# Streaming encoder step: the order of the last convolution norms, the queue of their stores, and the place of the samples' loads

## The chip, the cores and the metric

The kernel runs on one core of a Trainium2 chip. The core has four compute engines that each work through a queue of their own in order: TensorE (PE: matrix products and transposes; its weight loads are listed as PEld), VectorE (DVE), ScalarE (ACT) and GpSimd (POOL). They wait for each other by semaphores. SyncE (SP) computes nothing here and issues most DMA transfers, also in order; GpSimd's queue issues some. The metric is the device time of one execution in microseconds (us), lower is better.

## The reference

One step of a streaming encoder layer, in float32, for a new stream of 2048 frames (the prompt) and for 8 running streams of 16 frames (the samples). What this case touches is the first sub-layer, the mixer. Attention and convolution share one input projection:

```python
proj = h @ w_in
q, k, v, u_val, u_gate = jnp.split(proj, [D_ATT, 2 * D_ATT, 3 * D_ATT, 3 * D_ATT + D_CONV], axis=-1)
...
att = band_attention(pad(q), k_ext, v_ext, key_valid, rel_bias)[:, :T]
...
u = u_val * jax.nn.sigmoid(u_gate)
u_ext = jnp.concatenate([conv_buf, u], axis=1)
c = lax.conv_general_dilated(u_ext, conv_w[:, None, :], window_strides=(1,), padding="VALID",
    dimension_numbers=("NWC", "WIO", "NWC"), feature_group_count=D_CONV) + conv_b
c = jax.nn.silu(layernorm(c, cln_g, cln_b))
...
y = jnp.concatenate([att, c], axis=-1) @ w_out
```

D_MODEL is 1024, D_ATT and D_CONV are 512, the convolution is 31 frames wide, and there are 8 heads of 64 with a relative-position bias in the softmax. A prompt query sees its own chunk of 64 keys and 8 chunks before it; a sample sees 256 cached keys and its 16 new ones. Cross-attention into 256 memory tokens and a SwiGLU network of 2816 follow. The step also returns the new key, value and convolution rows.

## The kernel before

Tokens stand in tiles of 128: tiles 0 to 15 are the prompt, and one more (the sample tile) holds the 8 x 16 frames of the samples. The program has stages: memory projections, `phase_proj` (the mixer's input projection and the convolution), `attention`, the output projection, cross-attention, and the feed-forward network. Matrix products are exact to float32 by a split of each operand in a high and a low part, three products each (`mm3`, lines 283 to 285).

`phase_proj` runs over three groups of tiles. The last group is tiles 12 to 15 and the sample tile. In each group come values, then the convolution's inputs, then `qk(which, j, blk, x)`: keys (which = 1) and queries (which = 0) for the channel block j of 4, for x = 0 (three prompt tiles, products 384 wide) and x = 1 (the rest, 256 wide). The results go to DRAM arrays `ks` and `qs` (L717), and keys also to the output (L716, L714).

The depthwise convolution is done on VectorE (L523), and for the samples on ScalarE and GpSimd (L532, L533). Its steps stand in the Python lists `vq` and `pq`; `pump` draws one step at a time while the products are written. When all four channel blocks of a group (`cts`) are done, `conv_norm` does a LayerNorm and swish on each tile. Its steps, in order, are:

- four transposes on PE (L538), statistics on DVE (L540, L542), the reciprocal root on POOL (L298, L301);
- normalization on DVE (L546);
- four transposes back on PE (L550), scale and bias four times on ACT (L553, into buffer `z`, of which there are two), tanh on ACT (L556), the last product on DVE (L557), and the store of `cs[t]` to DRAM by SP (L558), 256 KB.

The tile's norms of the last group were put in `vq` in pairs: those of tiles 12 to 15 as the group begins, that of the sample tile at the end.

In `attention`, units of one head and one tile follow one another: `scores` (L856) with its softmax (L793 on DVE, L795 on ACT), transposes (L873) and products with the values (L886). With head h, the generator `sample(h)` handles sample h for all heads: it loads the cached keys `kt` (L800), cached values `vc` (L802) and new values `vn` (L804), appends the new keys on POOL (L806), lays out queries on DVE (L811), and computes scores (L816), softmax with the bias `bs` (L793, 272 wide), and products (L835). `head_load` (L780, L781) brings a head's queries, keys and values into SBUF; for head h + 1 it is written six units into head h. The bias `bs` is loaded once in eight parts of 16 rows (L899), to a place that the convolution's buffers had; the memsets L903 and the buffer of L890 are on such places too.

A scheduler of the tile framework puts the instructions of each engine into one order before the run. The program bends it by `issue_after(ins)`: an instruction within it comes behind `ins` in the order. PSUM is in tagged regions: in `phase_proj`, "mm" for products, "tr" for transposes and "ca" for the convolution's sums.

## Time and profile before

| | us |
|---|---|
| time before, median of 3 runs | 2971.57 (2968.06 to 2972.08) |
| the profiled execution's own time | 2970.86 |
| its span, first to last instruction | 2969.1 |
| TensorE busy in the span | 2877.8 (97%) |
| VectorE busy | 2076.6 (70%) |
| GpSimd busy | 1367.9 (46%) |
| ScalarE busy | 1308.7 (44%) |

The span starts with the first instruction and ends with the last; the execution's own time has 1.8 us around it. A row of a timeline has the start, the duration, the engine, the line, the operation, what it writes and reads, how often it ran in a row, and in brackets how long the engine had been idle before it and what ended the idle time. "SPq" marks an instruction that SP issues for a DMA; its duration is that of the issue, not of the transfer. The last convolution products of `phase_proj` are at about 615 us, and attention begins at 641 us.

### The profile page before, as it was taken

The numbers are of one execution on the slowest core, as the hardware profiler recorded it, in microseconds if no ns is written. First come the engines' busy times: TensorE is split into PE (matmuls) and PEld (weight loads), VectorE is DVE, ScalarE is ACT, GpSimd is POOL, SyncE is SP. The second block draws the span as 40 slices with busy tenths as digits, with TensorE's granted clock in tenths as the row PEclk, the third lists the DMA queues.
The fourth block names the chain that finished last, engine by engine and source line by source line (L and its number), as shares of the span: only waits on it lengthen the run. The fifth ranks groups of instructions, "written<-read, shape, count | busy, mean of one in ns | idle before, by whom it ended". The sixth has DMA issues, their size and how long they took to land.

```text
span 2969.1 us, 45382 instructions
## 1 busy us (share of the span) xinstructions
PE 2877.8 (97%) x16740; PEld 2628.1 (89%) x16740; DVE 2076.6 (70%) x3024; ACT 1308.7 (44%) x2661; POOL 1367.9 (46%) x1247
## 2 busy tenths in 40 slices
PE   8999999979989998999999999999999999999998
PEld 8999999968978776888879999999999999888786
DVE  6697795958985334445459888787888998546655
ACT  4535354648973223333334333433344444433433
POOL 0268395720022223145447656365656775424413
PEclk9999999989999999999999999999999999999999
DMA  8635255557845664223355333644434446756654
GB/s 307 245 114 179 91 167 161 169 154 188 214 144 175 229 219 164 76 96 126 112 172 196 138 114 133 200 155 152 145 121 160 148 143 211 242 172 221 226 193 165
DMA packets 198474, 500.04 MB, mean 168 GB/s; under 512 B 18981, under 2 KB 87085, under 8 KB 189923
## 3 DMA queue, kind: packets, MB, share of 16 engines
q1 hardware_dynamic: 187931, 461.09, 48.2%
q0 software_dynamic: 10320, 36.05, 3.1%
q8 instruction: 131, 2.15, 0.3%
q14 instruction: 92, 0.75, 0.1%
HBM read 365.97 MB, written 141.81 MB: 171 GB/s over the span
## 4 chain that ended last, share of the span: by engine, by line
PE 42%; DMA 3%; POOL 2%; DVE 2%; issue 1%; ACT 0%; DVEq 0%; SPq 0%; POOLq 0%; ACTq 0%
PE psb L285 13%; PE psb L284 13%; PE psb L283 13%; PE psb L291 1%; DMA sbf<-in_w_down_dram 1%; DMA sbf<-x 1%; POOL sbf L1500 1%; PE psb L1355 1%; DMA sbf<-hn 1%; POOL sbf L340 0%; DVE sbr L1378 0%; DMA hn<-sbf 0%; DVE flexb L1440 0%; DVE sbr L1561 0%; DVE sbx L1378 0%
## 5 line engine op out<-in xcount | busy, mean ns | idle before, releaser
L283 PE MATMUL psb<-sbr 128*128 128x384 f32 (+3 forms) x2808 | 942.1, 337 | 3.3 <-ACT sbr L319 1.1
L284 PE MATMUL psb<-sbr 128*128 128x384 f32 (+3 forms) x2356 | 805.6, 342 | 2.4 <-DVE sbr L320 2.4
L285 PE MATMUL psb<-sbr 128*128 128x512 f32 (+3 forms) x1848 | 632.7, 344 | 2.2 <-DVE sbr L1561 2.2
L283 PEld LDWEIGHTS psb<-sbr 128*128 128x128 f32 x2808 | 530.5, 189 | 32.5 <-ACT sbr L1357 1.7
L285 PE MATMUL psb<-sbr,sbx 128*128 128x384 f32 (+2 forms) x1484 | 476.8, 322 | 0.0
L284 PEld LDWEIGHTS psb<-sbr 128*128 128x128 f32 x2356 | 445.0, 189 | 29.4 <-DVE sbr L320 2.7
L285 PEld LDWEIGHTS psb<-sbr 128*128 128x128 f32 x1848 | 348.0, 189 | 30.6 <-DVE sbr L1561 4.2
L291 PE MATMUL psb<-sbr 128*128 128x512 f32 x1226 | 304.6, 397 | 12.5 <-ACT sbr L319 8.5
L1378 DVE TENSOR_TENSOR sbr<-sbf,sbr 128x512 fp32r<-128x512 f32 x258 | 263.3, 1023 | 38.0 <-ACT sbr L1377 37.2
L291 PEld LDWEIGHTS psb<-sbr 128*128 128x128 f32 x1226 | 227.8, 189 | 64.1 <-ACT sbr L319 9.0
L1377 ACT CAST sbr<-sbf 128x512 fp32r<-128x512 f32 x258 | 159.3, 620 | 277.3 <-PE psb L284 235.7
L285 PEld LDWEIGHTS psb<-sbr,sbx 128*128 128x128 f32 x1484 | 280.6, 189 | 0.2
L523 DVE SCALAR_TENSOR_TENSOR psb<-sbf,psb 128x768 f32<-128x768 f32 (+1 forms) x290 | 264.3, 912 | 6.2
L1561 DVE TENSOR_TENSOR sbr<-sbf,sbr 128x384 fp32r<-128x384 f32 (+1 forms) x231 | 163.0, 728 | 96.6 <-ACT sbr L1560 95.3
L278 POOL TENSOR_TENSOR sbx<-sbf,sbr 128x1024 fp32r<-128x1024 f32 x60 | 152.1, 2537 | 78.3 <-ACT sbr L277 73.7
L1560 ACT CAST sbr<-sbf 128x384 fp32r<-128x384 f32 (+1 forms) x231 | 111.0, 497 | 167.6 <-PE psb L284 146.2
L1500 POOL TENSOR_TENSOR sbf<-sbf 128x512 f32<-128x512 f32 x77 | 107.3, 1399 | 166.6 <-DMA sbf<-in_w_down_dram 165.1
L533 POOL TENSOR_TENSOR flexb<-flexb,flexb 128x128 f32<-128x128 f32 (+1 forms) x180 | 167.2, 929 | 21.3 <-ACT flexb L532 11.7
L283 PE MATMUL psb<-sbr,sbx 128*128 128x384 f32 (+1 forms) x524 | 170.5, 327 | 0.7 <-ACT sbr L1357 0.7
L1377 ACT CAST sbx<-sbf 128x512 fp32r<-128x512 f32 x153 | 94.7, 620 | 160.5 <-PE psb L284 151.1
L1378 DVE TENSOR_TENSOR sbx<-sbf,sbx 128x512 fp32r<-128x512 f32 x153 | 151.8, 994 | 15.0 <-ACT sbx L1377 14.6
L1372 POOL TENSOR_TENSOR sbf<-sbf 128x512 f32<-128x512 f32 x66 | 97.4, 1476 | 109.5 <-DVE sbr L1378 51.3
(322 smaller groups left out, 5910.4 us busy)
## 6 DMA issues: line engine op xcount, KB each, us to landing
af<-flexb SPq DMA_DIRECT2D x33, 1344.0 KB, 6.2
sbf<-in_w_down_dram SPq DMA_DIRECT2D x154, 256.0 KB, 3.7
sbf<-af SPq DMA_DIRECT2D x90, 384.0 KB, 4.0
sbf<-in_w_gate_dram SPq DMA_DIRECT2D x66, 512.0 KB, 3.3
sbf<-in_w_up_dram SPq DMA_DIRECT2D x66, 512.0 KB, 3.3
sbf<-x SPq DMA_DIRECT2D x49, 512.0 KB, 3.9
sbf<-in_w_in_dram SPq DMA_DIRECT2D x48, 512.0 KB, 3.9
sbr<-ks SPq DMA_DIRECT2D x28, 512.0 KB, 10.1
```

Of the source, the lines that this page charges most:

```text
L278: self.lo_engine.tensor_tensor(lo[:, :], wf[:, :], hi[:, :].bitcast(F32), ALU.subtract)
L283: nc.tensor.matmul(ps, lh, rh, start=start, stop=False, **kw)
L284: nc.tensor.matmul(ps, lh, rl, start=False, stop=False, **kw)
L285: nc.tensor.matmul(ps, ll, rh, start=False, stop=stop, **kw)
L291: nc.tensor.matmul(y[o], l, r[:, o * 512:(o + 1) * 512], start=start and x == 0, stop=stop and x == 2)
L523: nc.vector.scalar_tensor_tensor(acc if w < CW - 1 else o, src(w), cwt[:, j, w:w + 1], acc, ALU.mult, ALU.add)
L533: nc.gpsimd.tensor_tensor(o, o, v, ALU.add)
L1377: nc.scalar.copy(hs[j][:, :], src[j])
L1378: nc.vector.tensor_tensor(ls[j][:, :], src[j], hs[j][:, :].bitcast(F32), ALU.subtract)
L1500: nc.gpsimd.tensor_tensor(acc[:, :], acc[:, :], q[:, :], ALU.add if s > 0 else ALU.subtract)
L1560: nc.scalar.copy(ch[:, m], a[:, x, m])
L1561: nc.vector.tensor_tensor(cl[:, m], a[:, x, m], ch[:, m].bitcast(F32), ALU.subtract)
```

## The change

The change does three things.

First, the five norms of the last group are no longer drawn from `vq`. When the last channel block's projections begin, the lists of convolution steps are emptied, the five `conv_norm` generators are made, with a PSUM tag "nt" of their own, and their steps are written behind each of the four last `qk` calls: one step each of tiles 12 and 13 behind the first; a second step of these and the first of tiles 14 and 15 behind the second; and so on. `issue_after` puts them behind the last product written so far.

Second, the `cs` stores of these five norms are issued by GpSimd's queue instead of SP's.

Third, a sample's three loads are issued on SP behind the last load of its head (for sample 0: behind the last store of `ks` or `qs` written).

```diff
-        nc.tensor.matmul(ps, ll, rh, start=False, stop=stop, **kw)
+        self.last_product = nc.tensor.matmul(ps, ll, rh, start=False, stop=stop, **kw)
...
-        ps_mm = ps_tr = Region().lay(self.ps, 0, ("mm", 2, 4), ("tr", 2, 2), ("ca", 4, 1))
+        ps_mm = ps_tr = Region().lay(self.ps, 0, ("mm", 2, 4), ("tr", 2, 2), ("ca", 4, 1)).lay(self.ps, 12, ("nt", 2, 2))
...
-        def conv_norm(t, cts, off):
-            pt = self.t(ps_tr, [P, 4, P], F32, "tr")
+        def conv_norm(t, cts, off, tag="tr"):
+            pt = self.t(ps_tr, [P, 4, P], F32, tag)
...
-            nc.sync.dma_start(self.cs[t], z[:, :, :].rearrange("p a b -> p (a b)"))
+            (nc.sync if tag == "tr" else nc.gpsimd).dma_start(self.cs[t], z[:, :, :].rearrange("p a b -> p (a b)"))
...
-            if last:
-                vq += pairs(tiles[:-1], cts)
-
...
-                nc.sync.dma_start(dst[:, :, col:col + npc].rearrange("c p n -> p c n"),
-                                  sp[:, :, :npc].bitcast(F32))
+                self.last_load = nc.sync.dma_start(dst[:, :, col:col + npc].rearrange("c p n -> p c n"),
+                                                   sp[:, :, :npc].bitcast(F32))
...
+            if last:
+                while vq or pq:
+                    pump(vq or pq, 1)
+                norms = [conv_norm(t, cts, i * P, "nt") for i, t in enumerate(tiles)]
+
+            def behind(*steps):
+                with self.tc.issue_after(self.last_product.ins):
+                    for i, n in steps:
+                        for _ in range(n):
+                            next(norms[i], None)
+
             for x in range(2):
                 for w in (1, 0):
                     qk(w, 3, blks[w], x)
+                    if last:
+                        behind(*[((0, 1), (1, 1)), ((0, 2), (1, 2), (2, 1), (3, 1)),
+                                 ((2, 2), (3, 2), (4, 1)), ((4, 2),)][2 * x + 1 - w])
...
-            if last:
-                vq += pairs(tiles[-1:], cts, len(tiles) - 1)
...
-        nc.sync.dma_start(v2[:, a:b, :].bitcast(F32), self.vs[h // 4][:, h % 4, a:b, :])
+        return nc.sync.dma_start(v2[:, a:b, :].bitcast(F32), self.vs[h // 4][:, h % 4, a:b, :])
...
-            nc.sync.dma_start(kt[:, :, :PAST], A["cache_att_kt"][s].rearrange("p (c k) -> p c k", k=PAST))
             vc = self.t(pool, [P, 2, 512], F32, "vc", 2)
-            nc.sync.dma_start(vc[:, :, :], A["cache_att_v"][s].rearrange("(b p) d -> p b d", p=P))
             vn = self.t(pool, [DEC_S, 512], F32, "vn", 2)
-            nc.sync.dma_start(vn[:, :], self.vsamp[s * DEC_S:(s + 1) * DEC_S, :])
+            with self.tc.issue_after(self.last_load.ins):
+                nc.sync.dma_start(kt[:, :, :PAST], A["cache_att_kt"][s].rearrange("p (c k) -> p c k", k=PAST))
+                nc.sync.dma_start(vc[:, :, :], A["cache_att_v"][s].rearrange("(b p) d -> p b d", p=P))
+                nc.sync.dma_start(vn[:, :], self.vsamp[s * DEC_S:(s + 1) * DEC_S, :])
...
-                    self.head_load(h + 1, heads[h + 1], 0, NPT)
+                    self.last_load = self.head_load(h + 1, heads[h + 1], 0, NPT)
```

Line numbers move: after the change L707 is L704, L714 is L711, L716 is L713, L717 is L714, L780 is L789, L781 is L790, L800 is L812, L802 is L813, L804 is L814, L806 is L816, L811 is L821, L816 is L826, L820 is L830, L856 is L866, L873 is L883, L899 is L909, L903 is L913, and the softmax L793 and L795 are L802 and L804. Lines up to 558 keep their numbers.

The order of the instructions moves in three places. On TensorE, where the convolution ends before the change, the norms' transposes (L538, L550) of tiles 12 to 15 stand together, and 48 products of 384 columns (L283 to L285) come behind them:

```order
L538 MATMUL psb<-ident_73,flexb_157 128x128 x2
L550 MATMUL psb<-ident_73,flexb_153 128x128 x8
L538 MATMUL psb<-ident_73,flexb_157 128x128 x8
L550 MATMUL psb<-ident_73,flexb_153 128x128 x4
L707 MATMUL psb<-ident_73,sbf 128x128 x3
L283 MATMUL psb<-sbr 128x384
L284 MATMUL psb<-sbr 128x384
L285 MATMUL psb<-sbr,sbx 128x384
```

After the change, on TensorE at the end of the projections and the beginning of attention, the rows are these (L866 are scores):

```order
L285 MATMUL psb<-sbr,sbx 128x256
L866 MATMUL psb<-sbr 128x256 x4
L866 MATMUL psb<-sbr 128x128 x2
L550 MATMUL psb<-ident_73,flexb_153 128x128 x4
L538 MATMUL psb<-ident_73,flexb_157 128x128 x4
L550 MATMUL psb<-ident_73,flexb_153 128x128 x4
L538 MATMUL psb<-ident_73,flexb_157 128x128 x4
L866 MATMUL psb<-sbr 128x512 x2
L866 MATMUL psb<-sbr 128x384 x2
L704 MATMUL psb<-ident_73,sbf 128x128
L866 MATMUL psb<-sbr 128x384 x2
L538 MATMUL psb<-ident_73,flexb_157 128x128 x4
```

All products are now ahead, and the norms stand among the scores of the first units; ahead of the piece shown, only the first transposes of tiles 12 and 13 stand among the 256 products. In both programs 18 score products stand ahead of sample 0's scores.

On GpSimd, at the same place, before the change:

```order
L301 TENSOR_TENSOR flexb_157<-flexb_157,mhalf_78 128x1
L298 TENSOR_SCALAR flexb_157<-flexb_157 128x1
L301 TENSOR_TENSOR flexb_157<-flexb_157,mhalf_78 128x1
L806 COPY sbf<-flexb_153 128x4x16 x2
L298 TENSOR_SCALAR flexb_157<-flexb_157 128x1
L301 TENSOR_TENSOR flexb_157<-flexb_157,mhalf_78 128x1
L903 MEMSET flexb_153 128x128 x2
L806 COPY sbf<-flexb_153 128x4x16
L820 TENSOR_SCALAR flexb_153<-flexb_153,flexb_157 128x272
```

On GpSimd after the change (cs_32 to cs_36 are the rows of tiles 12, 13, 14, 15 and the sample tile):

```order
L558 DMA cs_32_104<-flexb_153 128x512
L298 TENSOR_SCALAR flexb_157<-flexb_157 128x1
L301 TENSOR_TENSOR flexb_157<-flexb_157,mhalf_78 128x1
L558 DMA cs_33_105<-flexb_153 128x512
L913 MEMSET flexb_153 128x128 x2
L816 COPY sbf<-flexb_153 128x4x16
L558 DMA cs_34_106<-flexb_153 128x512
L558 DMA cs_35_107<-flexb_153 128x512
L558 DMA cs_36_108<-flexb_153 128x512
L830 TENSOR_SCALAR flexb_153<-flexb_153,flexb_157 128x272
```

The five stores now stand in this queue, and the copy of a sample's new keys (L816) is ahead of the last three; that copy writes a buffer that sample 0's scores read.

On SP, from the value load of head 1 (L781), before the change:

```order
L781 DMA sbr<-vs_18_90 128x2048
L717 DMA ks_17_89<-sbf 128x2x384
L558 DMA cs_35_107<-flexb_153 128x512
L780 DMA sbr<-qs_10_82 64x2048
L780 DMA sbr<-ks_14_86 64x2048 x2
L716 DMA out_dram<-sbf 128x512 x3
L717 DMA qs_13_85<-sbf 128x2x384
L717 DMA ks_17_89<-sbf 128x2x128
L716 DMA out_dram<-sbf 128x512
L714 DMA out_dram<-sbf 8x16x512
L802 DMA flexb_157<-in_cache_att_v_dram 128x2x512
L780 DMA sbr<-ks_14_86 64x2048
```

On SP at the same place after the change:

```order
L789 DMA sbr<-qs_10_82 64x2048 x2
L789 DMA sbr<-ks_14_86 64x2048
L713 DMA out_dram<-sbf 128x512 x2
L714 DMA qs_13_85<-sbf 128x2x384
L789 DMA sbr<-ks_14_86 64x2048 x2
L713 DMA out_dram<-sbf 128x512
L789 DMA sbr<-ks_14_86 64x2048
L714 DMA ks_17_89<-sbf 128x2x128
L790 DMA sbr<-vs_18_90 128x2048
L812 DMA sbf<-in_cache_att_kt_dram 128x4x256
L814 DMA sbf<-vsampd_149 16x512
L714 DMA qs_13_85<-sbf 128x2x128
```

The next row there is the second L812, the keys of sample 0; the first is that of sample 1. Both key loads (L800 before) stood ahead of the first piece; the `cs` stores are gone from this queue; and head 1's six loads now stand in one piece ahead of its values.

## The prediction

> **What bounds the kernel now.** I read the busy line of the page first, then a table of busy time by stage, then TensorE's timeline where that table shows a hole, then what the last instructions of the hole wait for.
>
> ```profile
> PE 2877.8 (97%) x16740; PEld 2628.1 (89%) x16740; DVE 2076.6 (70%) x3024; ACT 1308.7 (44%) x2661; POOL 1367.9 (46%) x1247
> ...
> 600.00:615.00 15.00, 15.00 (x117) 15.00 (x116) 13.98 (x22) 8.80 (x26) 8.81 (x20) 1.00 0.21 72
> ...
> 610.00:680.00 70.00, 46.00 (x266) 37.15 (x264) 34.52 (x79) 31.20 (x91) 7.00 (x18) 0.80 0.56 151
> 640.00:670.00 30.00, 16.03 (x88) 11.46 (x88) 13.28 (x38) 13.89 (x43) 1.77 (x7) 0.88 0.96 237
> ...
> 680.00:840.00 160.00, 159.50 (x1248) 145.23 (x1242) 147.42 (x359) 144.73 (x348) 7.78 (x22) 1.00 0.87 212
> ```
>
> After the times of a stretch and its length come PE, PEld, DVE, ACT and POOL busy, then granted clock, share of the DMA engines and GB/s. TensorE is full up to 615 us and from 680 us on. Between 610 and 680 us it is busy 46.00 of 70.00 us: **24.0 us of idle time**, all that this change can reach, since the changed steps lie there. The page counts 2877.8 busy of a span of 2969.1, so this one hole is a quarter of all TensorE idle time. Its clock there is 0.80, a further loss that I leave unpriced.
>
> ```profile
> 615.19 0.44 PE L538 MATMUL psb<-ident,flexb 128*128 128x128 f32 x2
> 619.07 1.97 PE L550 MATMUL psb<-ident,flexb 128*128 128x128 f32 x8 [3.45 <-DVE flexb L546]
> 621.78 1.11 PE L538 MATMUL psb<-ident,flexb 128*128 128x128 f32 x4 [0.74 <-ACT flexb L553]
> 623.18 1.12 PE L538 MATMUL psb<-ident,flexb 128*128 128x128 f32 x4 [0.28 <-ACT flexb L553]
> 626.05 1.12 PE L550 MATMUL psb<-ident,flexb 128*128 128x128 f32 x4 [1.76 <-DVE flexb L546]
> 628.29 1.47 PE L707 MATMUL psb<-ident,sbf 128*128 128x128 f32 x3 [1.12 <-DVE flexb L546]
> ...
> 655.57 0.80 PE L856 MATMUL psb<-sbr 128*128 128x256 f32 x2 [3.81 <-ACT flexb L695]
> 656.55 1.13 PE L816 MATMUL psb<-sbf,flexb 128*32 128x272 f32 x8 [0.19 <-issue]
> ...
> 662.78 0.87 PE L856 MATMUL psb<-sbr 128*128 128x384 f32 x4 [0.93 <-DVE flexb L793]
> ...
> 670.38 1.01 PE L856 MATMUL psb<-sbr 128*128 128x384 f32 x2 [4.81 <-DVE flexb L793]
> 672.65 2.78 PE L856 MATMUL psb<-sbr 128*128 128x384 f32 x8 [1.26 <-DVE flexb L793]
> ...
> 678.54 0.65 PE L835 MATMUL psb<-flexb,sbf 128*32 128x128 f32 x16 [0.88 <-ACT sbf L827]
> ```
>
> The bracket is idle time before a group and what ended it. The hole has two halves. First the norms of tiles 12 to 15 (L538 and L550): TensorE waits in the middle of its queue for their DVE and ACT steps, 3.45 + 0.74 + 0.28 + 1.76 + 1.12 = 7.35 us, with the last 48 projection products still behind them. Then attention starts late and waits for loads. The longest wait, 4.81 us, goes back to VectorE:
>
> ```profile
> 655.11 0.69 DVE L557 SCALAR_TENSOR_TENSOR flexb<-flexb 128x512 f32<-128x512 f32 x1 [0.23 <-ACT flexb L556]
> ...
> 669.88 0.44 DVE L793 CUSTOM_DVE_ANT_0 flexb<-psb,flexb 128x272 f32<-128x272 f32 x1 [5.22 <-DMA flexb<-toep]
> ...
> 615.21 0.57 SPq L800 DMA_DIRECT2D sbf<-in_cache_att_kt_dram  x1
> 624.45 6.38 SPq L558 DMA_DIRECT2D cs<-flexb  x3
> ...
> 638.92 0.65 SPq L780 DMA_DIRECT2D sbr<-qs  x1
> ...
> 655.83 12.45 SPq L899 DMA_DIRECT2D flexb<-toep  x8
> ```
>
> The 128x272 softmax of sample 0 needs the sample bias. Its eight small loads (L899) overwrite the convolution's buffers, so they start at 655.83, when the last norm step (L557) is done, and SP needs 12.45 us to issue them, since it also waits for head 1's loads, of which this is the first (638.92).
>
> **Part 1: the products come ahead of the norms.** By the order, 83 products of 384 columns and 56 of 256 stand ahead of the transposes that need the last convolution channel, against 35 and 96 before, after the same predecessors. That is 48 more of 384 and 40 fewer of 256.
>
> ```profile
> 615.00 0.28 PE L285 MATMUL psb<-sbr,sbx 128*128 128x256 f32 x1
> ...
> 633.05 0.33 PE L285 MATMUL psb<-sbr,sbx 128*128 128x384 f32 x1
> 633.22 0.33 PE L283 MATMUL psb<-sbr 128*128 128x384 f32 x1
> ```
>
> A 384 product follows the last by 0.17 us; a 256 product, from 614.88 to 615.00 in the same view, by 0.12. So these transposes come at 615.19 + 48 x 0.174 - 40 x 0.12 = 618.7, still behind the end of the convolution (about 615.2), hence without a wait. The last 384 product is eight 256 products earlier, at 617.8. Forty more 256 products (4.8 us) follow, with five transposes: the projections end at about 624.4, not past 640. The 7.35 us of waits go, but not for good: the norms now stand among the first scores, and what decides is what comes late next.
>
> **Part 2: sample 0's keys become late.** Head 1's loads may start when the last 384 product has read the weights, at 617.8 instead of 638.92. By SP's order, between that point and the end of sample 0's key load there are six head loads (0.524 MB each), the value load (1.049), three key outputs (0.786 together), three stores of q and k (0.655), two key loads (1.049) and a small one: 6.7 MB. In before the key load was issued at 615.21, ahead of all that. At 237 GB/s, which 640:670 shows at a DMA share of 0.96, it takes 28.4 us; with the landing of a small load (2.5, below) the keys arrive at 617.8 + 28.4 + 2.5 = 648.7. Sample 0's scores (L816, after: L826) follow the 18th score product in both programs, 656.55 before and about 648.7 after, and take 1.13: 649.8. Ahead of them TensorE has nothing to do for some 10 us: this wait takes the place of the old ones. Bounds: at the 289 GB/s of 650:660, below, the keys would come 5 us earlier; at the 212 of the full stretch 680:840, 3 us later.
>
> ```profile
> 650.00:660.00 10.00, 5.33 (x26) 3.59 (x27) 4.58 (x14) 3.37 (x10) 0.24 (x1) 0.66 1.07 289
> ```
>
> **Part 3: the stores on GpSimd's queue.** No convolution store stood there before. Its nearest rows are GpSimd's other stores (issue durations, then landing), the SP store that it replaces, and the small bias loads:
>
> ```profile
> L1285 POOL DMA_DIRECT2D hn<-sbf x9: 534/544/573, 1313.8 to 1599.6; - x9
> DMA to landing us min/median/max: 2.4/3.2/5.4
> ...
> L1059 POOL DMA_DIRECT2D x<-flexb x17: 571/628/680, 922.7 to 1172.5; - x17
> DMA to landing us min/median/max: 2.9/5.1/10.0
> ...
> L558 SPq DMA_DIRECT2D cs<-flexb x17: 319/326/1167, 330.6 to 668.3; - x17
> DMA to landing us min/median/max: 2.0/2.7/5.0
> ...
> L899 SPq DMA_DIRECT2D flexb<-toep x8: 302/302/420, 655.8 to 667.9; - x8
> DMA to landing us min/median/max: 1.7/2.5/10.3
> ```
>
> A store is 256 KB, as L1285's. It may cost 2.4 (the shortest) to 10.0 us (the longest, of a 512 KB store); I take **5 us**, near L1285's longest, since SP's queue is full at that time. The first stores hide under the wait for keys, also at 10: the third norm's ACT step reuses the buffer of the first and waits for its store's landing; the first norm needed 9.3 us from its transposes to its store in before (615.19 to 624.45), so from 618.7 its store is due at 628 and lands by 638, and the keys come at 648.7. What is new is GpSimd's order: a copy of sample 2's new keys (0.24), into the buffer that sample 0's scores read, stands ahead of the third store (cs14), and behind it stand the stores of tile 15 and the sample tile. GpSimd waits at that copy for those scores. So cs14 is issued at 650.2 and lands at 655.2; only then may the sample tile's L553 refill the buffer (four times, 1.50 us in before), and TensorE's transposes wait for ACT: 656.7. Nothing hides these 5 us; each further microsecond is lost one for one. The five issues cost GpSimd some 0.6 us each; it idles there (7.00 busy of 70.00), so nothing.
>
> The Trainium skill, page "DMA: Bandwidth & Descriptors", section "Queues, rings and completion order", says that a DMA engine takes turns between queue rows packet by packet; section "Anatomy of one DMA" fits 2.0 us plus bytes over 436 GB/s, an estimate of 2.6 for 256 KB. By that cs14 lands 2.4 us earlier, which is the first rival; L1285's median of 3.2 with a longest of 5.4 lies above the page.
>
> **The sum.** In both programs 18 score products stand ahead of sample 0's scores, and TensorE gets past these at 656.55 in before; after, it goes on at 656.7. From there before still loses 0.19 + 0.93 + 4.81 + 1.26 + 0.88 = 8.07 us. After, the sample tile's L557 ends about 1.3 us behind L553, at 658.0; eight issues of 0.30 and a landing of 2.5 bring the bias at 662.9, as head 1's loads have long landed. Between that L557 and the softmax of sample 0 VectorE has three conversions (L875, after: L885) and two softmax passes (L793, after: L802):
> ```profile
> L793 DVE CUSTOM_DVE_ANT_0 flexb<-psb,flexb 128x640 f32<-128x640 f32 (+5 forms) x14 | 9.7, 695 | 10.6 <-DMA flexb<-toep 5.2 <-PE psb L856 3.8 <-ACT sbf L710 1.3
> L875 DVE TENSOR_TENSOR sbx<-psb,sbx 128x512 fp32r<-128x512 f32 (+3 forms) x6 | 3.2, 554 | 3.3 <-ACT sbx L874 3.3
> L793 DVE DVE_READ_ACCUMULATOR2_ANT flexb<- 128x1 f32 x14 | 1.1, 82 | 0.0
> ```
>
> That is 3 x 0.55 + 2 x 0.78 = 3.2 us, 661.2 at the earliest, so up to 1.7 us are left to wait for the bias; its work waits for TensorE in between, and I count 0.6. Gain: 8.07 - 0.6 = 7.5 us. The profiled execution took 2970.86 us (1.8 outside its span), 0.7 under the median: 2970.86 - 7.5 = 2963.4; by the median 2964.1. I say **2963**, as the clock of 0.80 in the hole may recover a little.
>
> **Part 4: the other samples' loads** now follow the value load of the head. In the full stretch 680:840 TensorE idles 0.5 us of 160, with a key load issued a head (27 us) before its use; 1 MB ahead of it is 4.7 us at 212 GB/s. I cost it at nothing; that slack hides it. Without it each of six heads could lose the 4.7.
>
> **Rivals.**
> - *Light landings.* GpSimd's stores land in 3 us, as the median of L1285, and the keys come at 289 GB/s, up to 5 us earlier. TensorE then goes on 2 to 6 us sooner: about 2959. For it: the queues are separate. Against it: a DMA share of 0.96 to 1.07 in this stretch.
> - *The gain is given back.* cs14 takes 8 to 10 us as the worst of L1059, and the keys come 1 to 2 us later: 4 to 7 us of the 7.5 go, about 2969. For it: both transfers run in the busiest DMA stretch. This holds also the case that the change does not do what it says, since the bytes to move (151 GB/s x 70 us, 10.6 MB) set the end: 2971. Against that: DMA share is 0.56 over the hole, and the loads start 21 us sooner.
> - *Slower: key load and cs14 in a row.* One chain, head 1's 6 MB ahead of the keys, then scores, copy and store. At 166 GB/s (660:670, whose row has share 0.78) the keys need 40.5 us, 12.1 more than counted; with a landing of 10.0, 5 more. 17.1 - 7.5 = 9.6 us slower: about 2980. It decides from 7.5 us of added lateness, when the keys come at 656. Against it: 166 is a stretch in which the queue ran dry.
>
> ```profile
> 660.00:670.00 10.00, 4.63 (x32) 3.78 (x30) 3.14 (x9) 3.39 (x7) 0.00 (x0) 0.97 0.78 166
> ```
>
> **How the numbers follow.** The forecast gets 0.55 (2961 to 2967), light landings 0.15, the gain given back 0.21, slower 0.09. A measurement of this kernel can tell about 0.2%, 5.9 us, from no change: faster is under 2965.6, slower over 2977.5. Of the forecast 0.45 lies under that bound and 0.10 within; with the first rival that is 0.60 faster, 0.31 within, 0.09 slower. The range reaches from an early cs14 with faster keys (2957) to a landing of 10 with late keys (2973); the slower case is left out.
>
> **What would show it.** Right: no L538 wait between 615 and 625; the projections' last products at 624; head 1's first load issued near 618; a TensorE wait of about 10 us ended by the key load near 649; cs14 landing about 5 us after; sample 0's 128x272 softmax at 661 to 663; TensorE full from there. Wrong: keys before 645 or after 653, cs14 landing outside 3 to 8, a third wait behind the bias loads, or idle time in later heads ended by key loads.

## The result, and the profile after

| | before | after |
|---|---|---|
| time, median (range), us | 2971.43 (2968.06 to 2972.08), 4 runs | 2954.55 (2953.77 to 2956.82), 4 runs |
| profiled execution, us | 2970.86, span 2969.1 | 2955.24, span 2953.5 |
| TensorE busy / idle in the span, us | 2877.8 / 91.3 | 2873.3 / 80.2 |

The ratio is 0.9947 (95% interval 0.9931 to 0.9962): the changed kernel is 16.9 us faster, more than twice the 7.5 us of the forecast and below the range of 2957 to 2973.

Where the 15.6 us between the two spans lie is read from one table of busy time for each kernel. Its stretches are cut at the same instructions, as the count of TensorE's matmuls, the first in each row, shows (some records are missing). Only at the first cut does the order differ a little: 3 products of 384 columns stand on one side of it in place of 3 of 256, worth under 0.2 us. After the times and the length come busy time of PE, PEld, DVE, ACT and POOL, granted clock, DMA share and GB/s. Before:

```profile
610.00:720.00 110.00, 86.00 (x574) 74.33 (x573) 70.60 (x169) 67.82 (x179) 8.50 (x22) 0.88 0.67 172
...
835.00:870.00 35.00, 32.24 (x232) 28.57 (x231) 29.67 (x75) 26.88 (x65) 11.15 (x8) 0.95 0.40 137
...
1150.00:2969.10 1819.10, 1777.68 (x9560) 1624.34 (x9560) 1272.42 (x1705) 695.66 (x1352) 911.76 (x776) 0.99 0.47 160
```

After:

```profile
610.96:708.00 97.04, 80.55 (x576) 71.53 (x575) 70.53 (x166) 65.81 (x170) 11.43 (x27) 0.88 0.67 186
...
823.00:854.45 31.45, 30.55 (x232) 27.01 (x231) 29.61 (x75) 26.78 (x65) 11.64 (x8) 1.00 0.49 169
...
1134.50:2953.50 1819.00, 1779.38 (x9560) 1623.37 (x9560) 1271.08 (x1705) 694.94 (x1352) 910.25 (x775) 0.99 0.47 159
```

Two stages changed. The one with the hole takes 97.04 instead of 110.00 us: **13.0 us**. Another, 115 us later, takes 31.45 instead of 35.00: **3.55 us**, in a place where the prediction expected nothing. The long last stretch is equal within 0.1 us, as are the two left out. The profiled execution of after only comes 0.96 us later into the hole (610.96 against 610.00); this difference stands already at 580 us, ahead of the changed steps. So 0.96 - 12.96 - 3.55 - 0.1 = -15.6.

TensorE's timeline in the hole, after the change:

```profile
643.06 1.11 PE L550 MATMUL psb<-ident,flexb 128*128 128x128 f32 x4 [4.45 <-ACT flexb L553]
646.08 1.14 PE L826 MATMUL psb<-sbf,flexb 128*32 128x272 f32 x8 [1.91 <-DMA sbf<-in_cache_att_kt_dram]
652.71 0.48 PE L883 MATMUL psb<-ident,flexb 128*128 128x128 f32 x1 [4.87 <-ACT flexb L553]
654.30 1.11 PE L883 MATMUL psb<-ident,flexb 128*128 128x128 f32 x4 [1.11 <-DVE sbx L885]
661.47 0.66 PE L883 MATMUL psb<-ident,flexb 128*128 128x128 f32 x4 [0.29 <-ACT flexb L804]
663.54 0.85 PE L866 MATMUL psb<-sbr 128*128 128x384 f32 x4 [0.50 <-DVE flexb L802]
```

The waits of before among the norms are gone, but for some of 1.3 us and less ahead of the rows shown. Three long waits have come: 4.45 us for the third norm, 1.91 for the keys, 4.87 for the sample tile's norm. What they wait for stands in the timelines of SP, GpSimd, ScalarE and VectorE:

```profile
618.07 1.09 SPq L789 DMA_DIRECT2D sbr<-qs  x2
...
636.34 0.57 SPq L812 DMA_DIRECT2D sbf<-in_cache_att_kt_dram  x1
...
633.82 0.69 POOL L558 DMA_DIRECT2D cs<-flexb  x1 [3.24 <-DVE flexb L557]
...
647.30 0.26 POOL L816 COPY sbf<-flexb 128x64 f32<-128x64 f32 x1 [3.29 <-PE psb L826]
647.54 0.54 POOL L558 DMA_DIRECT2D cs<-flexb  x1
...
641.50 2.92 ACT L553 ACTIVATE flexb<-psb,sbf 128x128 f32<-128x128 f32 x8 [2.37 <-DMA cs<-flexb]
651.15 1.50 ACT L553 ACTIVATE flexb<-psb,sbf 128x128 f32<-128x128 f32 x4 [2.90 <-DMA cs<-flexb]
...
659.02 0.44 DVE L802 CUSTOM_DVE_ANT_0 flexb<-psb,flexb 128x272 f32<-128x272 f32 x1 [0.34 <-DMA flexb<-toep]
```

Head 1's loads start at 618.07. The first store (tile 12) is issued at 633.82 and ScalarE, which refills its buffer, goes on at 641.50: 7.7 us. cs14 is issued at 647.54, right behind GpSimd's copy, and ScalarE goes on at 651.15: 3.6 us. The softmax of sample 0 runs at 659.02 instead of 669.88. How the DMA engines fare in the same stage:

```profile
610.00:680.00 70.00, 53.69 (x363) 47.14 (x362) 44.91 (x104) 41.25 (x112) 10.55 (x24) 0.83 0.60 174
...
620.00:630.00 10.00, 9.67 (x78) 8.95 (x76) 7.23 (x20) 3.79 (x15) 2.88 (x9) 1.00 1.03 268
630.00:640.00 10.00, 5.76 (x24) 3.76 (x22) 6.13 (x13) 5.91 (x17) 3.04 (x5) 0.69 1.01 280
640.00:650.00 10.00, 2.87 (x14) 1.23 (x14) 2.89 (x9) 4.44 (x11) 1.72 (x5) 0.50 0.96 355
650.00:660.00 10.00, 6.18 (x34) 5.67 (x34) 4.74 (x11) 5.60 (x14) 0.54 (x1) 0.62 0.27 86
...
670.00:680.00 10.00, 10.00 (x77) 9.57 (x77) 8.44 (x23) 9.18 (x22) 0.00 (x0) 1.00 0.64 136
680.00:840.00 160.00, 159.32 (x1261) 144.56 (x1261) 148.28 (x362) 144.94 (x349) 13.22 (x26) 1.00 0.85 216
```

The engines are full for 30 us (1.03, 1.01, 0.96) and almost empty from 650 on (0.27). TensorE stands behind this burst. Between 610 and 680 us it is now busy for 53.69 instead of 46.00 us, and it is full from 664 instead of 680.

**The second stage.** Here is the end of the wait in before (TensorE, GpSimd, SP, and the busy table right behind):

```profile
842.79 0.55 PE L825 MATMUL psb<-ident,flexb 128*128 128x128 f32 x3 [1.87 <-POOL flexb L820]
840.76 1.04 POOL L277 CAST sbr<-sbf 128x1024 fp32r<-128x1024 f32 x1 [8.77 <-issue]
841.77 0.96 POOL L820 TENSOR_SCALAR flexb<-flexb,flexb 128x272 f32<-128x272 f32 x1
822.35 0.53 SPq L802 DMA_DIRECT2D flexb<-in_cache_att_v_dram  x1
832.48 0.33 SPq L273 DMA_DIRECT2D sbf<-in_w_out_dram  x1
...
842.80:846.20 3.40, 3.40 (x17) 3.28 (x18) 1.52 (x3) 2.25 (x6) 0.00 (x0) 0.59 0.00 0
```

A sample's softmax is scaled on GpSimd (L820). In GpSimd's queue it stands behind the rounding of an output weight (L277), which waits for the weight's load. This load was issued at 832.48, about 10 us behind the sample's value load, and the rounding starts 8.3 us later. TensorE waits 1.87 us, and for 3.4 us behind it works at a clock of 0.59. The row of the rounding in before names no releaser ("issue"); that it waits for the weight is read from the same row after the change, in e1 and in e4, which name it. In the table by stage the idle time of this stretch is 2.76 us before and 0.90 after (1.86 less), busy time 32.24 and 30.55 (1.69 less): the wait and the clock. After the change:

```profile
826.52 1.04 POOL L277 CAST sbr<-sbf 128x1024 fp32r<-128x1024 f32 x1 [7.08 <-DMA sbf<-in_w_out_dram]
827.54 0.97 POOL L830 TENSOR_SCALAR flexb<-flexb,flexb 128x272 f32<-128x272 f32 x1
798.36 0.61 SPq L813 DMA_DIRECT2D flexb<-in_cache_att_v_dram  x1
820.50 0.34 SPq L273 DMA_DIRECT2D sbf<-in_w_out_dram  x1
```

The value load is issued at 798.36, right behind the sample's keys, and no longer stands in the burst ahead of the weight; the rounding starts 6.0 us after its load's issue, 2.3 us less than before. The value load is 0.52 MB, and at the 212 GB/s of the full stretch 680:840 that is an estimate of 2.5 us. The DMA share from the weight's issue to the rounding is 1.00 in before (832.50:840.80) and 0.79 after (820.50:826.50). TensorE does not wait for the scaling.

### The profile page after: what moved, and what is told of

Same layout as the page of the kernel before. It is cut to its first block, busy times and chain, and to the rows that moved or that the text cites. A ratio compares the mean times of both kernels' runs of the same rounds, so it can differ in the third digit from the quotient of the medians.

```text
span 2953.5 us, 45369 instructions
## 1 busy us (share of the span) xinstructions
PE 2873.3 (97%) x16740; PEld 2623.8 (89%) x16740; DVE 2078.6 (70%) x3024; ACT 1307.3 (44%) x2661; POOL 1370.9 (46%) x1252
## 4 chain that ended last, share of the span: by engine, by line
PE 42%; DMA 3%; POOL 2%; DVE 2%; issue 1%; ACT 0%; DVEq 0%; SPq 0%; POOLq 0%; ACTq 0%
PE psb L285 13%; PE psb L284 13%; PE psb L283 13%; DMA sbf<-in_w_down_dram 1%; PE psb L291 1%; DMA sbf<-x 1%; POOL sbf L1510 1%; PE psb L1365 1%; DMA sbf<-hn 0%; DVE sbr L1388 0%; POOL sbf L340 0%; DMA hn<-sbf 0%; DMA sbf<-in_w_gate_dram 0%; DVE sbr L1571 0%; DVE flexb L1450 0%
## 5 line engine op out<-in xcount | busy, mean ns | idle before, releaser
L283 PE MATMUL psb<-sbr 128*128 128x384 f32 (+3 forms) x2808 | 942.7, 337 | 5.8 <-ACT sbr L1570 1.8
L285 PE MATMUL psb<-sbr 128*128 128x512 f32 (+3 forms) x1848 | 632.8, 344 | 2.6 <-DVE sbr L1571 2.5
L283 PEld LDWEIGHTS psb<-sbr 128*128 128x128 f32 x2808 | 530.3, 189 | 36.1 <-ACT sbr L1570 3.3
L285 PE MATMUL psb<-sbr,sbx 128*128 128x384 f32 (+2 forms) x1484 | 476.8, 322 | 0.0
L285 PEld LDWEIGHTS psb<-sbr 128*128 128x128 f32 x1848 | 348.1, 189 | 32.0 <-DVE sbr L1571 5.2
L285 PEld LDWEIGHTS psb<-sbr,sbx 128*128 128x128 f32 x1484 | 280.7, 189 | 0.3
L283 PE MATMUL psb<-sbr,sbx 128*128 128x384 f32 (+1 forms) x524 | 170.5, 327 | 1.2 <-ACT sbr L1367 0.7
L1388 DVE TENSOR_TENSOR sbx<-sbf,sbx 128x512 fp32r<-128x512 f32 x153 | 153.2, 1003 | 15.6 <-ACT sbx L1387 15.4
```

The source lines that it names most:

```text
L283: nc.tensor.matmul(ps, lh, rh, start=start, stop=False, **kw)
L285: self.last_product = nc.tensor.matmul(ps, ll, rh, start=False, stop=stop, **kw)
L1388: nc.vector.tensor_tensor(ls[j][:, :], src[j], hs[j][:, :].bitcast(F32), ALU.subtract)
```

## The experiments

Each kernel was timed in five rounds beside the kernel before on the same chip (e1 to e4 on one, e5 to e8 on a second, e9 to e11 on a third), and the ratio is to those runs of before. Beside the ratio stand two numbers worked out from the traces: by how much the **hole** and the **second stage** became shorter than in before. They are the differences in start time of the same TensorE instructions, ahead of a stage and behind it. For the changed kernel they are 13.0 and 3.6. In e5 and e6 TensorE loses about 1 us at 572 us already, 40 us ahead of the hole, in a wait of 0.78 and 1.05 us for a copy on GpSimd, where its order is that of the changed kernel; this is not counted as part of the hole.

The theory at the outset: the norm order makes the gain in the hole, and the stores' own queue makes it possible. The rivals: the order alone makes it; or the sample loads do.

**e1, the sample loads as in before** (with the norm order and GpSimd's stores):

```diff
-            with self.tc.issue_after(self.last_load.ins):
-                nc.sync.dma_start(kt[:, :, :PAST], ...)
+            nc.sync.dma_start(kt[:, :, :PAST], ...)
```

> The changed kernel with the samples' loads left where they were (norm order and GpSimd stores alone). Theory 1 (the trace after): the hole at the phase change closes by the norm order, 13 us of the gain; the samples' loads cost about 2 us there, since the keys of sample 0 come behind head 1's loads, and win about 3.6 us late in attention, where GpSimd waits at 840 us for an output-weight load that a sample's value load had been ahead of. So here: no wait for the keys of sample 0, the stall of about 1.9 us before the transposes of a sample near 840 us of before is back; 2971.4 - 13 - 2 = about 2956. Rival (the three parts work only together, keys ahead change nothing): as the changed kernel without its late gain, 2958 to 2959, with a TensorE wait of the same length ahead of sample 0's scores ended by something else. Second rival (the loads' place is worth nothing): 2954.5.

Measured: 2962.86 us, 0.998 (0.997 to 0.9991). Hole 11.8 shorter, second stage 2.2. TensorE's waits:

```profile
641.44 1.12 PE L550 MATMUL psb<-ident,flexb 128*128 128x128 f32 x4 [5.62 <-ACT flexb L553]
...
650.51 0.47 PE L882 MATMUL psb<-ident,flexb 128*128 128x128 f32 x1 [5.99 <-ACT flexb L553]
...
829.17 0.55 PE L834 MATMUL psb<-ident,flexb 128*128 128x128 f32 x3 [1.13 <-POOL flexb L829]
...
1171.91 1.09 PE L318 MATMUL psb<-ident,sbf 128*128 128x128 f32 x8 [1.53 <-DVE sbr L1258]
```

With the early keys there is no wait for keys, and the two waits for the stores grow (5.62 and 5.99). The hole gains nearly as much. In the second stage a wait of 1.13 us is left. The total is worse by more than the two stages, for a reason outside them: without this part of the change the program's order in the cross attention comes out another way too, with a new wait of 1.53 us at 1171.91, and 4.2 us are lost there. The kernels e4 and e6 have the same other order there (some 7 and 4 us lost); the others have that of before, but for a few instructions. The same wait stands in all three (1.53, 1.55 and 1.54 us); in e4 alone the clock fell behind it, to 0.70 over ten us, and e4 loses some 3 us more. So these three are read by stage, not by total.

**e2, the stores back on SP's queue:**

```diff
-            (nc.sync if tag == "tr" else nc.gpsimd).dma_start(self.cs[t], ...)
+            nc.sync.dma_start(self.cs[t], ...)
```

> The changed kernel with the last group's convolution stores back on SP's queue (norm order and samples' loads alone). Theory 1: SP takes its queue in order, and the first store stands behind head 1's loads, the keys and the key outputs, so it is issued near 641 instead of 634 us and lands near 645 to 649; the third norm's scale step on ACT, which waits for that landing, comes 4 to 8 us later, the end of the hole with it: 2958 to 2963, with an ACT wait ended by that store of 6 us or more. Rival (the queue of the stores is worth nothing, as the keys come at 646 anyway): within 1 us of 2954.5.

Measured: 2953.56 us, 0.9953 (0.9939 to 0.9966). Hole 12.7 shorter, second stage 3.6.

```profile
647.21 1.12 PE L550 MATMUL psb<-ident,flexb 128*128 128x128 f32 x4 [9.59 <-ACT flexb L553]
...
652.30 0.48 PE L883 MATMUL psb<-ident,flexb 128*128 128x128 f32 x1 [1.58 <-ACT flexb L553]
...
645.65 1.51 ACT L553 ACTIVATE flexb<-psb,sbf 128x128 f32<-128x128 f32 x4 [7.51 <-DMA cs<-flexb]
```

The theory fell here: the queue is worth nothing that can be measured. The first store is late on SP (issued at 638.26), and TensorE waits 9.59 us in one piece instead of 4.45 + 1.91 + 4.87 in three, but it goes on at 652.30 against 652.71.

**e3, the norm order alone** (both edits above):

> The norm order alone, stores on SP, the samples' loads where they were. Theory 1: the losses of both other parts: first store late (4 to 8 us), keys early (2 us won), the stall near 840 us there: 2971.4 - 13 + 4 to 8 - 2 = 2960 to 2965. Rival (most of the gain needs the other queue): 2968 or more. Rival (the order is all): 2955 to 2957.

Measured: 2956.48 us, 0.9962 (0.9947 to 0.9976). Hole 12.6 shorter, second stage 2.0, with a wait of 1.25 us for the scaling left in it. The order alone brings nearly the whole gain of the hole. It also brings 2.0 of the 3.6 us of the second stage, though the wait there is only 0.6 us shorter than in before: the clock behind it stays at 1.00 (828:838), and the 1.7 us that before lost to the low clock are not lost.

**e4, the sample loads alone:** the kernel before, with the loads moved as in the change.

> The kernel before with only the samples' loads issued behind the loads of their head. Theory 1: the stall near 840 us goes (3.6 us with the low clock behind it); at the phase change sample 0's scores stand later in TensorE's order, and the bias loads end no earlier, so that part stays within 3 us: 2965 to 2971. Rival (what my prediction counted, the loads' place is worth nothing in attention): 2970 to 2972 with the wait of 1.9 us near 840 us still there.

Measured: 2973.71 us, 1.002 (1.0011 to 1.0029). Hole 1.3 us longer, second stage 3.3 shorter, some 7 lost in the cross attention. Neither total that was expected came. The hole has a new wait, and the second stage has none for the scaling:

```profile
670.27 1.14 PE L817 MATMUL psb<-sbf,flexb 128*32 128x272 f32 x8 [7.41 <-DMA sbf<-in_cache_att_kt_dram]
...
839.44 1.04 POOL L277 CAST sbr<-sbf 128x1024 fp32r<-128x1024 f32 x1 [6.41 <-DMA sbf<-in_w_out_dram]
840.45 0.97 POOL L821 TENSOR_SCALAR flexb<-flexb,flexb 128x272 f32<-128x272 f32 x1
```

So the moved loads are what removes the wait of the second stage; what they are worth there is 3.3 us by themselves, and 1.3 to 1.6 beside the norm order (the change and e2 against e1 and e3), with which the low clock is gone already. In the hole they cost 1.3 us by themselves; in the change that cost is at least partly covered by the waits for the stores (e1 and e8, where the keys come early, have a hole 1.2 us longer and 1.1 to 1.5 shorter).

The next kernels take away what is left in the hole, from the changed kernel. The theory: each wait for itself costs its length. The rival: the DMA burst sets the end, and whatever is taken away, the next landing is met.

**e5, head 1's loads behind the bias loads:**

```diff
+            bs_load = nc.sync.dma_start(bs[h * DEC_S:(h + 1) * DEC_S, :], toep[h][...])
...
+                    with self.tc.issue_after(bs_load.ins):
+                        self.last_load = self.head_load(h + 1, heads[h + 1], 0, NPT)
```

> The changed kernel with one thing more: head 1's loads (4.2 MB) are issued on SP behind the sample bias loads, so that they are no longer ahead of the keys of sample 0 nor beside the convolution stores. Theory 2: what ends the hole in the changed kernel is DMA landings (the first store took 7.7 us, the keys came at 646, the third store 3.6 us), and these are late for head 1's bytes. Then stores land in about 3 us, the keys are there at 635, and the bias is in place about 8 us sooner than at 659 us: 2945 to 2949, with TensorE waits of less than 3 us ended by stores and keys. Rival (the bytes have to come anyway, the wait only moves): the same hole, or a new wait of head 1's first scores near 670 to 690 us ended by head 1's loads: 2952 to 2957. Second rival (the chain of ACT, DVE and TensorE steps of the five norms sets the end, not landings): less than 2 us off.

Measured: 2953.74 us, 0.9948 (0.9935 to 0.996). Hole 13.2 shorter.

```profile
647.37 0.47 PE L883 MATMUL psb<-ident,flexb 128*128 128x128 f32 x1 [4.07 <-ACT flexb L553]
...
670.18 0.59 PE L866 MATMUL psb<-sbr 128*128 128x128 f32 x3 [2.35 <-DMA sbr<-ks]
```

TensorE goes on 5.3 us sooner (647.37), and loses it again where head 1's scores wait for their keys (2.35, and once more 2.03 at 695.80, with a clock of 0.83 from 690 to 700). The rival holds: the wait moves.

**e6, a third buffer for the norms** (so the third norm need not wait for the first store):

```diff
-                   .lay(fa, 0, ("xn", 2, 2), ("z", 2, 2), ...
+                   .lay(fa, 0, ("xn", 2, 2), ("zz", 2, 2), ...
+                   .at("z", 2, (fa, [4, 6, 26]))
```

> The changed kernel with a third buffer z for the convolution's last steps, so that the third norm's scale step waits for no store, the fourth for the first store and the sample tile's for the second. Theory 2: the waits of 4.45 and 4.87 us that ACT's scale steps end go, the wait for the keys of sample 0 (to 646 us) takes up the first; the bias comes when the sample tile's norm is done, 3 to 4 us sooner than at 659: 2950 to 2952. Rival (the bytes on the DMA engines between 620 and 650 us set the end, whichever buffer waits): within 1 us of 2954.5.

Measured: 2956.1 us, 0.995 (0.9937 to 0.9962). Hole 14.4 shorter, 1 to 1.4 us more than in the changed kernel (13.0, and 13.4 in e11), with 4 us lost in the cross attention. The waits of 4.45 and 4.87 us for the stores are gone, and the wait for the keys takes most of their place:

```profile
645.30 1.14 PE L827 MATMUL psb<-sbf,flexb 128*32 128x272 f32 x8 [6.45 <-DMA sbf<-in_cache_att_kt_dram]
```

**e7, e5 and e6 together:**

> Head 1's loads behind the bias loads, and the third buffer. Theory 2: neither stores nor keys are waited for, the five norms run through behind the projections and the bias is in place near 648 us, 11 us sooner than in the changed kernel: 2942 to 2946. Rival (bytes): 2952 to 2957, with a wait of head 1's scores. Rival (norm steps): as the run with head 1's loads late alone.

Measured: 2952.09 us, 0.9936 (0.9923 to 0.9948). Hole 14.4 shorter. The softmax of sample 0 comes at 650.78, 8 us sooner than after the change, but head 1's queries and keys are now waited for (2.09 and 2.11 us), and from 660 to 670 TensorE is busy for 5.79 of 10 us.

**e8, the loads of samples 0 and 1 as in before, the others moved:**

```diff
-            with self.tc.issue_after(self.last_load.ins):
+            with self.tc.issue_after(self.last_load.ins) if s > 1 else nullcontext():
```

> The changed kernel, but the loads of samples 0 and 1 stay where they were (keys ahead of head 1's loads); the later samples' loads are behind those of their head as in the change. Theory 2: the keys of sample 0 are not waited for, but the landings of the stores still are (as in the run without the samples' part, where 5.62 and 5.99 us took the place of 4.45, 1.91 and 4.87), so the phase change is worth the same within 1.5 us, and the stall near 840 us of before is gone: 2953 to 2956. Rival (the wait for the keys was 1.9 us of the path): 2951 to 2953.

Measured: 2953.68 us, 0.9947 (0.9933 to 0.996). Hole 14.5 shorter. Ahead of sample 0's scores TensorE is idle for 0.21 us, and not for the keys; the store waits are 6.49 and 3.92. By this run the late keys cost the change 1.1 to 1.5 us in the hole, of the 1.91 that TensorE waits for them; e1, where the keys are early as well, gained only 11.8 there, so the cost is not settled to better than that.

**e9, e6 and e8 together:**

> The changed kernel with the keys of sample 0 ahead of head 1's loads (samples 0 and 1 free) and the third buffer z. Theory 3 (several landings stand in a row at the hole, and each edit so far took away one and met the next): with neither keys nor stores waited for, and head 1's loads still early, the waits of 4.45, 1.91 and 4.87 us go and no wait of head 1's scores comes near 665: phase change 4 to 6 us better than in the changed kernel, 2948 to 2951. Rival (the DMA engines' bytes set the end whatever the order): 2952 to 2955, with TensorE waiting for another landing between 640 and 700 us.

Measured: 2950.86 us (2947.83 to 2952.95), 0.9935 (0.9921 to 0.9948). Hole 16.3 shorter, second stage 3.6. One long wait is left, and it is a store's landing still (TensorE, then ScalarE):

```profile
642.27 0.69 PE L885 MATMUL psb<-ident,flexb 128*128 128x128 f32 x2 [4.19 <-ACT flexb L555]
...
640.71 2.90 ACT L555 ACTIVATE flexb<-psb,sbf 128x128 f32<-128x128 f32 x8 [2.98 <-DMA cs<-flexb]
```

By the trace this is the best version: 3 us more in the hole than the changed kernel, about the sum of what e6 and e8 bring singly. By the total it is 3.8 us ahead of e11 below, which ran beside it, but the two intervals of the ratio overlap, so the 3 us rest on the stage.

**e10, head 1's loads behind sample 0's keys, with the third buffer:**

> The changed kernel with the third buffer z and head 1's loads directly behind the keys of sample 0, not behind the bias. Theory 3: as the run before, but head 1's loads start some 10 us later (about 630), end near 652, and are not late for head 1's scores (which needed them near 665 in the run with both edits): 2947 to 2951. Rival (bytes): 2952 to 2955 with a wait of head 1's scores near 665 ended by head 1's loads.

Measured: 2953.02 us, 0.9947 (0.9934 to 0.9959). Hole 11.5 shorter. The waits ahead of 650 shrink, and a new one comes (TensorE, then VectorE):

```profile
659.53 1.01 PE L869 MATMUL psb<-sbr 128*128 128x384 f32 x2 [5.17 <-DVE flexb L803]
...
659.03 0.44 DVE L803 CUSTOM_DVE_ANT_0 flexb<-psb,flexb 128x272 f32<-128x272 f32 x1 [5.89 <-DMA flexb<-toep]
```

The bias loads overwrite the buffer of the last store. This store is issued at 646.12, and SP, which waits for its landing, can issue them at 654.03 only: 7.9 us, in a stretch that head 1's loads, moved behind the keys, now keep full (its DMA share is 1.00 from 650 to 654). The wait has moved from the keys to the bias.

**e11, the changed kernel again,** beside e9 and e10:

> The changed kernel once more, on the same chip as the two runs ahead, so that these are compared on one chip. All theories: 0.9947 of the kernel before within 0.0015; at the phase change waits of about 4.5, 1.9 and 4.9 us, none of 1.9 us near 830.

Measured: 2954.7 us (2951.49 to 2958.96), 0.9946 (0.9934 to 0.9959). Hole 13.4 shorter, second stage 3.5: the stages repeat to 0.4 us.

## Why the prediction was right in direction and wrong in size

The forecast gained 7.5 us, all in the hole. The traces show 13.0 us there and 3.55 in the second stage. Two steps failed. The sum of the hole was mis-sized by 5.5 us, in Parts 2 and 3 and in the work that it left out; with that alone the time would have been about 2958, just inside the stated range. And Part 4 put a term at nothing that was worth 3.55 us, which carried the time out of the range.

- **Part 1** held. There is no wait for the norms ahead of 629, the projections end at 625.7 (624.4 was said), head 1's loads start at 618.07 (617.8). e3 shows that this part alone shortens the hole by 12.6 of the 13.0 us.
- **Part 2** had the mechanism and was mis-sized: the keys were waited for, but until 646.08 and not 648.7. The forecast moved 6.7 MB at 237 GB/s, a rate of before in a stretch whose DMA share was 0.96; after, shares of 1.03, 1.01 and 0.96 went with 268, 280 and 355 GB/s. It lay inside the bounds given (5 us earlier to 3 later). That is 2.6 us.
- **Part 3** had the chain right: copy, cs14, landing, ScalarE, TensorE. The landing was taken as 5 us and was 3.6, 1.4 us less. The first store was issued at 633.82 (628 was said) and its landing took 7.7 us, to 641.5 (638); it was hidden all the same, since TensorE waited 4.45 us for it but the keys came later still. What was believed of the queue itself fell in e2: on SP the stores do as well.
- **The sum** put the point from which TensorE goes on at 656.7, and 656.55 in before; it was 652.71, 3.84 us ahead of before. That is the 2.6 and the 1.4 us above. From there to the end of the hole (720.0 before, 708.0 after) the forecast counted 8.07 - 0.6 us, by idle time alone. Of the 8.07 us, 0.19 lie ahead of 656.55, so 7.88 count. After had 1.11 + 0.29 + 0.50 us of waits, and 0.17 between 680 and 690, so 2.07 instead of 0.6 (the bias itself was waited for 0.34 us by VectorE). Its work behind that point was shorter by 2.34 us (TensorE is busy for 55.55 us from 656.55 to 720.0 in before, for 53.21 from 652.71 to 708.0 after): 1.13 are sample 0's scores, which in before still lay behind 656.55 and in after were done (the forecast set the start of a group on one side against its end on the other). The other 1.2 are put down to the clock that the forecast left unpriced, 1.00 from 670 to 680 where it was 0.69; no run shows them apart. 3.84 + 7.88 - 2.07 + 2.34 = 12.0, and with the late entry of 0.96 the 13.0.
- A warning on idle time as a sum: the idle time of the stage went from 24.0 to 16.5 us, a difference of 7.5, as forecast. It is chance: the idle time ahead of the point and behind it moved otherwise than was said. Its work also shrank from 86.00 to 80.55 us, and less of it now runs in the stretches of low clock (18.8 us in the ten-us rows with a clock of 0.69 or less in before, 14.8 after). How much of the 5.45 us the clock explains is not shown; but what was called unpriced was not small beside the term that was priced.
- **Part 4 failed outright.** It costed the other samples' loads at nothing, from a full stretch 680:840 and with an eye on key loads that come too late. The stretch ends 0.9 us ahead of a wait, and the loads did not bring a wait but removed one: 1.87 us at 840.92, with 1.7 us of low clock behind it. The transfer concerned was not the sample's but the output weight's, queued behind the sample's values, and the instruction that waited for it was on GpSimd, ahead of the softmax's scaling. e4, with the loads moved and the norms as before, has a second stage shorter by 3.3 us; e3, with the norms moved and the loads as before, by 2.0 with 1.25 us of wait left. So of the 3.55 us the loads bring 1.3 to 1.6 beyond what the order brings without them. The 1.7 us of low clock stand in the one trace of before, and whether the clock falls there each time is not shown. Why the weight comes somewhat sooner in e1 and e3 too (7.5 and 7.65 us from issue to rounding, 8.3 in before) stays open.
- **The signs.** None of those named as wrong appeared: the keys came between 645 and 653, cs14 landed within 3 to 8 us, and no later head waits for key loads. Of those named as right, the single wait of about 10 us came in pieces of 4.45 and 1.91, and the softmax of sample 0 at 659.02, ahead of 661 to 663. The list had no sign for a gain elsewhere.
- **The rivals.** Light landings named the direction in which the forecast failed in the hole (keys and store sooner, 2959), but it too had nothing in the second stage: its 2959 less 3.6 is 2955.4, the profiled time of after being 2955.24. The Trainium skill, page "DMA: Bandwidth & Descriptors", section "Anatomy of one DMA", gave an estimate of 2.6 us for cs14; the trace has 3.6, and 7.7 for the first store of the same size. The slower case and the one that gives the gain back did not come: sample 0's keys came at 646.08, ten us ahead of the point from which it decides.

What limits the hole now, by these runs, is the burst of transfers between 618 and 650. e5 to e8 and e10 each take one or two waits away and meet another landing: of the keys, of head 1's loads, of a store or of the bias. The third buffer (e6) and the early keys (e8) still give 1 to 1.5 us each, and both together 3 (e9); moving head 1's loads gives nothing (e5, e7 against e6) or costs (e10).

Not tried: the output weight's load or its rounding moved by itself, which would test the second stage without the sample loads; the cross attention held in one order for all kernels; and a hole with fewer bytes to move.

## What to carry to other kernels

Price a moved load at every transfer that was queued behind it, and follow each of these to the in-order queue that waits for it, not only to the load's own reader; and let the window that is to show slack end well past the last use, since a full stretch says nothing of the wait that begins where it ends. Where several transfers land in one burst, taking away one wait shows the next, so count the gain from where the engine goes on for good, in work as well as in idle time. Undo the parts of a change singly: here the order of the norms was nearly all of the hole, the queue of the stores nothing, and the loads paid off 200 us later.

## What the runs showed of the hardware

A wait of 1.87 us on TensorE was followed by 3.4 us at a granted clock of 0.59 (row 842.80:846.20), though TensorE was busy all that time. The same in e4, behind a wait of 1.55 us in the cross attention. But in e1 the clock stayed at 1.00 behind a wait of 1.13 us, and also behind one of 1.53 us at the same place of the cross attention (e6, with 1.54 us there, has 1.00 too). The row of e4, then the two of e1:

```profile
1185.00:1195.00 10.00, 10.00 (x37) 8.31 (x38) 8.11 (x11) 5.11 (x5) 0.00 (x0) 0.70 0.72 231
```

```profile
829.00:839.00 10.00, 9.83 (x89) 8.94 (x90) 8.25 (x20) 8.58 (x21) 3.51 (x3) 1.00 0.18 58
...
1171.90:1181.90 10.00, 9.99 (x52) 8.52 (x53) 7.74 (x11) 5.85 (x6) 0.00 (x0) 1.00 0.71 228
```

The Trainium skill, page "TensorE: Matmul & The Clock Gate", Part 1, tells of a clock that falls to half after an idle window of about 3.4 us. The waits of 1.87 and 1.55 us are shorter than that, and the clock fell all the same. With 1.55 us it fell and with 1.53 and 1.54 it did not, so the length of a wait alone does not decide it here; what does stays open. The loss behind the 1.87 us (1.69 us of busy time) was about as large as the wait itself.

In the four cases looked at, the landing of one and the same kind of store went with the load on the DMA engines and not with the queue that issued it. These are the stretches from the issue of tile 12's store and of cs14 to ScalarE's going on, after the change (the share is the last number but one):

```profile
633.80:641.50 7.70, 3.88 (x13) 2.75 (x13) 3.22 (x8) 2.70 (x8) 2.47 (x4) 0.50 1.03 336
647.50:651.20 3.70, 0.34 (x2) 0.00 (x0) 1.21 (x3) 0.42 (x2) 1.12 (x3) 0.50 0.59 224
```

7.7 us at a share of 1.03, 3.6 us at 0.59. In e2 the first store, issued by SP at 638.26, took 7.4 us to ScalarE's going on at 645.65, at a share of 1.06. In e10 the last store, issued by GpSimd, took 7.9 us at a share of 1.01 (646.12:654.03).
